# An interleave of two arrays: x in four tiles of 64 KiB rows in one buffer, y in column halves

## The chip, the cores and the metric

The kernel runs on one core of one Trainium2 chip. The metric is the device time of one execution, in microseconds, as the median of several runs. The core has a TensorE, a VectorE (DVE in the profile), a ScalarE (ACT), a GpSimd (POOL) and a SyncE (SP); this kernel computes on VectorE alone, and uses SP and ACT to issue transfers. The transfers run on 16 DMA engines that both issuing queues share. A tile in on-chip memory has 128 partitions; a "row" below is the stretch of one partition that one DMA moves, contiguous in HBM and on the chip.

## The reference

Two float32 arrays of shape 32 x 256 x 1024 are interleaved element by element along the last axis:

```
result = np.zeros((batch, seq, dim * 2), dtype=np.float32)
result[..., 0::2] = x
result[..., 1::2] = y
```

So 33.55 MB of x and 33.55 MB of y are read, and 67.11 MB are written. There is no arithmetic. Since the whole array is interleaved in the same manner, it may be cut anywhere as one flat sequence.

## The kernel before

The flat arrays are cut into n = 8 tiles of 128 partitions with W = 8192 floats each (32 KiB per partition, 4 MiB per tile of x and of y). Row p of tile k is contiguous in HBM, and the rows of a tile lie one behind another. The output of a tile is 64 KiB per partition; it is produced in two halves h of 32 KiB each, so that a store writes 32 KiB of every 64 KiB.

There are two buffers each for x (`xt`), y (`yt`) and output halves (`ot`), every one 32 KiB per partition; all six take 192 KiB of a partition.

Three engines work through lists of their own, which are written out by hand, and meet only in semaphores:

- SP issues all loads (lines 42 to 53), in the order x, y of each tile. From the third tile on, the load of x waits until the third of the four copies of the tile two before is done (L48, semaphore `woven`, which every copy raises by one), and that of y until the fourth is (L52): then the buffer is free. Tile 0's x comes as two halves (L42, L43), whose two DMAs are moved ahead of the barrier that opens the program (lines 103 to 122), so that they run before the other engines are ready.
- VectorE does two copies for each output half, x into the even columns (L67) and y into the odd ones (L70). Before the first of them it waits for the x tile, and for the earlier store from the same output buffer (`osem`); before the second, for the y tile.
- ACT issues a store as soon as both copies of a half are done (L74 and L83). The very first half goes out as two stores, of 8 and 24 KiB per partition (L77, L81), with a semaphore of its own, `qsem`, for the first.

Within a queue the DMAs are served in the order of issue. Loads are on one queue (q1 in the profile), stores on another (q10). Where both have work, each of the 16 engines alternates between them row by row: in the trace a 32 KiB row of a load is followed by a 32 KiB row of a store. A DMA is complete when, on each engine, a small record behind its eight rows has been served; that is what raises the semaphore.

The kernel ends when the last two stores have landed (L87 to L93).

Of the kernel before, what the change touches and what calls it, by code (L numbers as in the profile page):

```python
# [3 lines left out]


def _interleave(nc, x, y, out):
    P = 128
    W = 8192
    H = W // 2  # L10

    total = 1
    for s in x.shape:
        total *= s
    n = total // (P * W)
    assert n * P * W == total

    def rows(ap, names, k):
        flat = ap.rearrange("b s d -> (b s d)")
        return flat[k * names : (k + 1) * names].rearrange("(p w) -> p w", p=P)  # L20

    fp32 = mybir.dt.float32
    xt = [nc.alloc_sbuf_tensor(f"xt{b}", [P, W], fp32).ap() for b in (0, 1)]
    yt = [nc.alloc_sbuf_tensor(f"yt{b}", [P, W], fp32).ap() for b in (0, 1)]
    ot = [nc.alloc_sbuf_tensor(f"ot{b}", [P, W], fp32).ap() for b in (0, 1)]

    xsem = [nc.alloc_semaphore(f"xsem{b}") for b in (0, 1)]
    hsem = nc.alloc_semaphore("hsem")
    qsem = nc.alloc_semaphore("qsem")
    ysem = [nc.alloc_semaphore(f"ysem{b}") for b in (0, 1)]  # L30
    woven = nc.alloc_semaphore("woven")
    osem = [nc.alloc_semaphore(f"osem{b}") for b in (0, 1)]


    cuts = [0, W // 4, W]
    parts = [slice(a, b) for a, b in zip(cuts, cuts[1:])]

    xs = [rows(x, P * W, k) for k in range(n)]
    ys = [rows(y, P * W, k) for k in range(n)]
    os_ = [rows(out, 2 * P * W, k) for k in range(n)]  # L40

    nc.sync.dma_start(out=xt[0][:, :H], in_=xs[0][:, :H]).then_inc(xsem[0], 16)  # L42
    nc.sync.dma_start(out=xt[0][:, H:], in_=xs[0][:, H:]).then_inc(hsem, 16)  # L43

    for k in range(n):
        b = k % 2
        if k >= 2:
            nc.sync.wait_ge(woven, 4 * (k - 2) + 3)  # L48
        if k:
            nc.sync.dma_start(out=xt[b], in_=xs[k]).then_inc(xsem[b], 16)  # L50
        if k >= 2:
            nc.sync.wait_ge(woven, 4 * (k - 2) + 4)  # L52
        nc.sync.dma_start(out=yt[b], in_=ys[k]).then_inc(ysem[b], 16)

    for k in range(n):
        b = k % 2
        for h in (0, 1):
            c = slice(h * H, (h + 1) * H)
            if h == 0:
                nc.vector.wait_ge(xsem[b], 16 * (k // 2 + 1))  # L60
            elif k == 0:
                nc.vector.wait_ge(hsem, 16)
            if k:
                nc.vector.wait_ge(osem[h], 16 * k)
            if (k, h) == (1, 0):
                nc.vector.wait_ge(qsem, 16)
            nc.vector.tensor_copy(out=ot[h][:, 0::2], in_=xt[b][:, c]).then_inc(woven, 1)  # L67
            if h == 0:
                nc.vector.wait_ge(ysem[b], 16 * (k // 2 + 1))
            nc.vector.tensor_copy(out=ot[h][:, 1::2], in_=yt[b][:, c]).then_inc(woven, 1)  # L70

    for k in range(n):
        for h in (0, 1):
            nc.scalar.wait_ge(woven, 4 * k + 2 * h + 2)  # L74
            if (k, h) == (0, 0):
                for c in parts[:-1]:
                    nc.scalar.dma_start(  # L77
                        out=os_[k][:, c], in_=ot[h][:, c]
                    ).then_inc(qsem, 16)
                c = parts[-1]  # L80
                nc.scalar.dma_start(out=os_[k][:, c], in_=ot[h][:, c]).then_inc(osem[h], 16)  # L81
                continue
            nc.scalar.dma_start(  # L83
                out=os_[k][:, h * W : (h + 1) * W], in_=ot[h]
            ).then_inc(osem[h], 16)

    nc.scalar.wait_ge(osem[0], 16 * n)  # L87
    used = sorted(s.num for s in [*xsem, hsem, qsem, *ysem, woven, osem[0]])
    assert used == list(range(used[0], used[-1] + 1)), used
    nc.scalar.sem_clear(range(used[0], used[-1] + 1))  # L90
    nc.sync.nop(nofuse=True).wait_op(osem[1], 16 * n, "sem-ge").then_inc(
        osem[1], -16 * n
    )  # L93


def kernel(tc, x, y, out):
    nc = tc.nc
    tc.close()
    tc.compile()

    _interleave(nc, x, y, out)

    blocks = nc.main_func.blocks
    for engine in (mybir.EngineType.SP, mybir.EngineType.SP):
        opening = blocks[0].instructions
        at, moved = next(
            (b, i)
            for b in blocks[1:]
            for i in b.instructions
            if i.engine == engine and i.opcode == "DMACopy"  # L110
        )
        assert not (moved.sync_info and moved.sync_info.on_wait)
        body = at.instructions
        body.remove(moved)
        gate = next(
            n
            for n, i in enumerate(opening)
            if i.engine == engine and i.opcode == "Drain"
        )
        opening.insert(gate, moved)  # L120
        at.instructions = body
        blocks[0].instructions = opening


# [1 line left out]
_INS = ['x', 'y']  # L126
_OUTS = [((32, 256, 2048), 'float32')]


# [23 lines left out]
```

## Time and profile before

The three runs took 314.12, 314.23 and 314.33 us; the median is 314.23.

| | before |
|---|---|
| median of the runs | 314.23 us |
| the profiled execution's own time | 314.18 us |
| its span (first to last instruction) | 312.9 us |
| VectorE busy | 72.0 us (23%), 32 copies |
| loads (q1): rows and completion records, MB, share of 16 engines | 2448, 67.11, 50.1% |
| stores (q10): the same | 2448, 67.11, 49.7% |
| mean traffic over the span | 429 GB/s |
| VectorE idle before L67, waiting for stores | 206.5 us |
| VectorE idle before L70, waiting for y (once) | 12.3 us |
| first copy starts, first store issued | 7.33 us, 24.24 us |

How to read it: the span is the time from the first to the last instruction that the profiler saw; the execution takes a little longer. "DMA share" is the mean busy share of the 16 DMA engines in a stretch. The chain that ended last is followed backwards from the last instruction, at each step to what released it. Waiting times of an engine are put to what ended them. Idle time of VectorE costs nothing as such; what counts is whether the DMA engines have work. Over a short stretch the GB/s waver by some per cent, since a row is counted where it starts or ends.

### The profile page before, as it was taken

To read this page: it belongs to the slowest core of one execution; us is meant where nothing else is said; L and a number is where in the kernel's file an instruction comes from. 1 tells how busy PE (TensorE), PEld (TensorE's weight loads), DVE (VectorE), ACT (ScalarE), POOL (GpSimd) and SP (SyncE) were. 2 spreads that over 40 slices of the span, in tenths; PEclk is the share of its full clock that TensorE was granted. 3 is DMA by queue.
4 is the path that set the end of the run, shared out by engine and by line. 5 is a ranking of instruction groups with operands and counts; after the bars stand their busy time and mean duration, and the time that the engine had idled before them with its cause. 6 is when DMAs were issued, how large, how long until landed. Compare 5 with 4: busy or idle time off the path is not lost.

```text
span 312.9 us, 114 instructions
## 1 busy us (share of the span) xinstructions
DVE 72.0 (23%) x32; POOL 0.2 (0%) x4
## 2 busy tenths in 40 slices
DVE  0216000501305023050220503205032050415410
POOL 0000000000000000000000000000000000000000
DMA  8999999999999999999999999999999999999998
GB/s 337 467 402 436 436 402 419 452 457 415 427 444 411 461 402 469 402 469 402 469 402 465 406 440 432 423 448 402 469 402 469 402 469 402 469 402 448 423 423 381
DMA packets 4896, 134.22 MB, mean 429 GB/s; under 512 B 544, under 2 KB 544, under 8 KB 544
## 3 DMA queue, kind: packets, MB, share of 16 engines
q1 hardware_dynamic: 2448, 67.11, 50.1%
q10 hardware_dynamic: 2448, 67.11, 49.7%
HBM read 67.11 MB, written 67.11 MB: 429 GB/s over the span
## 4 chain that ended last, share of the span: by engine, by line
DMA 82%; DVE 12%; issue 0%
DMA out_dram<-ot 76%; DMA yt<-in_y_dram 6%; DVE ot L70 6%; DVE ot L67 6%
## 5 line engine op out<-in xcount | busy, mean ns | idle before, releaser
L67 DVE COPY ot<-xt 128x4096 f32<-128x4096 f32 x16 | 36.7, 2295 | 213.8 <-DMA out_dram<-ot 206.5
L70 DVE COPY ot<-yt 128x4096 f32<-128x4096 f32 x16 | 36.6, 2288 | 12.3 <-DMA yt<-in_y_dram 12.3
L137 POOL MEMSET const-bfloat16-1.0<- 128x1 bf16 x1 | 0.1, 103 | 0.0
L137 POOL MEMSET const-uint8-127<- 128x1 uint8 x1 | 0.1, 102 | 0.0
L137 POOL MEMSET const-float32-0.0<- 128x1 f32 x1 | 0.1, 100 | 0.2 <-issue 0.2
L137 POOL MEMSET const-float32-1.0<- 128x1 f32 x1 | 0.1, 99 | 0.0
## 6 DMA issues: line engine op xcount, KB each, us to landing
out_dram<-ot ACTq DMA_DIRECT2D x15, 4096.0 KB, 34.1
yt<-in_y_dram SPq DMA_DIRECT2D x8, 4096.0 KB, 41.5
xt<-in_x_dram SPq DMA_DIRECT2D x7, 4096.0 KB, 24.3
xt<-in_x_dram SPq DMA_DIRECT2D x2, 2048.0 KB, 9.5
out_dram<-ot ACTq DMA_DIRECT2D x1, 3072.0 KB, 32.8
out_dram<-ot ACTq DMA_DIRECT2D x1, 1024.0 KB, 16.3
```

The costliest lines, as they stand in the source:

```text
L67: nc.vector.tensor_copy(out=ot[h][:, 0::2], in_=xt[b][:, c]).then_inc(woven, 1)
L70: nc.vector.tensor_copy(out=ot[h][:, 1::2], in_=yt[b][:, c]).then_inc(woven, 1)
L137: nc = _bacc.Bacc("TRN2", target_bir_lowering=False, num_devices=1)
```

## The change

W becomes 16384, so there are n = 4 tiles of 64 KiB per partition for x and y each. x has one buffer of 64 KiB instead of two of 32, and each tile of x is loaded by one DMA with rows of 64 KiB. A tile of y comes as two column halves of 32 KiB per partition, each into a buffer of its own. The output of a tile is now 128 KiB per partition, and goes out in four quarters of 32 KiB, alternately from two buffers. All buffers together still take 192 KiB of a partition, and every copy still has 128 x 4096 elements.

The order of the loads is new. In the opening, x of tile 0 and the first half of y stand ahead of the opening barrier, in place of two halves of x; y's second half follows behind it. For every later tile SP waits for the fourth of the eight copies of the tile before and loads y's first half, waits for the seventh (the last that reads x) and loads x, waits for the eighth and loads y's second half. The very first store is cut in 8 and 24 KiB as it was. Rows of stores lie 128 KiB apart in HBM instead of 64, and rows of y 64 KiB apart instead of 32.

```diff
-    W = 8192
+    W = 16384
     H = W // 2
+    Q = W // 4
...
-    xt = [nc.alloc_sbuf_tensor(f"xt{b}", [P, W], fp32).ap() for b in (0, 1)]
-    yt = [nc.alloc_sbuf_tensor(f"yt{b}", [P, W], fp32).ap() for b in (0, 1)]
-    ot = [nc.alloc_sbuf_tensor(f"ot{b}", [P, W], fp32).ap() for b in (0, 1)]
+    xt = nc.alloc_sbuf_tensor("xt", [P, W], fp32).ap()
+    yt = [nc.alloc_sbuf_tensor(f"yt{b}", [P, H], fp32).ap() for b in (0, 1)]
+    ot = [nc.alloc_sbuf_tensor(f"ot{b}", [P, H], fp32).ap() for b in (0, 1)]
...
-    nc.sync.dma_start(out=xt[0][:, :H], in_=xs[0][:, :H]).then_inc(xsem[0], 16)
-    nc.sync.dma_start(out=xt[0][:, H:], in_=xs[0][:, H:]).then_inc(hsem, 16)
     for k in range(n):
-        b = k % 2
-        if k >= 2:
-            nc.sync.wait_ge(woven, 4 * (k - 2) + 3)
         if k:
-            nc.sync.dma_start(out=xt[b], in_=xs[k]).then_inc(xsem[b], 16)
-        if k >= 2:
-            nc.sync.wait_ge(woven, 4 * (k - 2) + 4)
-        nc.sync.dma_start(out=yt[b], in_=ys[k]).then_inc(ysem[b], 16)
+            nc.sync.wait_ge(woven, 8 * (k - 1) + 4)
+            nc.sync.dma_start(out=yt[0], in_=ys[k][:, :H]).then_inc(ysem[0], 16)
+            nc.sync.wait_ge(woven, 8 * (k - 1) + 7)
+        nc.sync.dma_start(out=xt, in_=xs[k]).then_inc(xsem, 16)
+        if k:
+            nc.sync.wait_ge(woven, 8 * (k - 1) + 8)
+        else:
+            nc.sync.dma_start(out=yt[0], in_=ys[k][:, :H]).then_inc(ysem[0], 16)
+        nc.sync.dma_start(out=yt[1], in_=ys[k][:, H:]).then_inc(ysem[1], 16)
...
+        for h in range(4):
+            j = 4 * k + h
+            o = ot[j % 2]
             if h == 0:
-                nc.vector.wait_ge(xsem[b], 16 * (k // 2 + 1))
+                nc.vector.wait_ge(xsem, 16 * (k + 1))
+            if j >= 2:
+                nc.vector.wait_ge(osem[j % 2], 16 * (j // 2))
+            if j == 2:
+                nc.vector.wait_ge(qsem, 16)
+            nc.vector.tensor_copy(
+                out=o[:, 0::2], in_=xt[:, h * Q : (h + 1) * Q]
+            ).then_inc(woven, 1)
+            if h % 2 == 0:
+                nc.vector.wait_ge(ysem[h // 2], 16 * (k + 1))
+            c = (h % 2) * Q
+            nc.vector.tensor_copy(
+                out=o[:, 1::2], in_=yt[h // 2][:, c : c + Q]
+            ).then_inc(woven, 1)
...
+    cuts = [0, H // 4, H]
+    for j in range(4 * n):
+        dst = os_[j // 4][:, (j % 4) * H : (j % 4 + 1) * H]
+        nc.scalar.wait_ge(woven, 2 * j + 2)
+        parts = [slice(a, b) for a, b in zip(cuts, cuts[1:])] if j == 0 else [slice(0, H)]
+        for c in parts[:-1]:
+            nc.scalar.dma_start(out=dst[:, c], in_=ot[j % 2][:, c]).then_inc(qsem, 16)
+        c = parts[-1]
+        nc.scalar.dma_start(out=dst[:, c], in_=ot[j % 2][:, c]).then_inc(osem[j % 2], 16)
```

In the prediction, L42, L44 and L47 are lines of the kernel after: the waits of SP ahead of y's first half, of x and of y's second half.

More of the change, by code (lines that the diff above doesn't have):

```diff
@@ L22, in _interleave @@
     fp32 = mybir.dt.float32
-    xt = [nc.alloc_sbuf_tensor(f"xt{b}", [P, W], fp32).ap() for b in (0, 1)]
-    yt = [nc.alloc_sbuf_tensor(f"yt{b}", [P, W], fp32).ap() for b in (0, 1)]
-    ot = [nc.alloc_sbuf_tensor(f"ot{b}", [P, W], fp32).ap() for b in (0, 1)]
-    xsem = [nc.alloc_semaphore(f"xsem{b}") for b in (0, 1)]
-    hsem = nc.alloc_semaphore("hsem")
+    xt = nc.alloc_sbuf_tensor("xt", [P, W], fp32).ap()
+    yt = [nc.alloc_sbuf_tensor(f"yt{b}", [P, H], fp32).ap() for b in (0, 1)]
+    ot = [nc.alloc_sbuf_tensor(f"ot{b}", [P, H], fp32).ap() for b in (0, 1)]
+    xsem = nc.alloc_semaphore("xsem")
     qsem = nc.alloc_semaphore("qsem")
@@ L32, in _interleave @@
     osem = [nc.alloc_semaphore(f"osem{b}") for b in (0, 1)]
-    cuts = [0, W // 4, W]
-    parts = [slice(a, b) for a, b in zip(cuts, cuts[1:])]
     xs = [rows(x, P * W, k) for k in range(n)]
@@ L55, in _interleave @@
+            nc.sync.dma_start(out=yt[0], in_=ys[k][:, :H]).then_inc(ysem[0], 16)
[6 more added lines that the diff above has]
+        nc.sync.dma_start(out=yt[1], in_=ys[k][:, H:]).then_inc(ysem[1], 16)
     for k in range(n):
-        b = k % 2
-        for h in (0, 1):
-            c = slice(h * H, (h + 1) * H)
+        for h in range(4):
+            j = 4 * k + h
+            o = ot[j % 2]
@@ L59, in _interleave @@
             if h == 0:
-                nc.vector.wait_ge(xsem[b], 16 * (k // 2 + 1))
[L61 to L65, printed above, removed]
-                nc.vector.wait_ge(qsem, 16)
[L67 to L85, printed above, removed]
@@ L87, in _interleave @@
-    nc.scalar.wait_ge(osem[0], 16 * n)
-    used = sorted(s.num for s in [*xsem, hsem, qsem, *ysem, woven, osem[0]])
+                nc.vector.wait_ge(xsem, 16 * (k + 1))
+            if j >= 2:
+                nc.vector.wait_ge(osem[j % 2], 16 * (j // 2))
+            if j == 2:
+                nc.vector.wait_ge(qsem, 16)
+            nc.vector.tensor_copy(
[3 more added lines that the diff above has]
+                nc.vector.wait_ge(ysem[h // 2], 16 * (k + 1))
@@ L89, in _interleave @@
+    nc.scalar.wait_ge(osem[0], 32 * n)
+    used = sorted(s.num for s in [xsem, qsem, *ysem, woven, osem[0]])
     assert used == list(range(used[0], used[-1] + 1)), used
     nc.scalar.sem_clear(range(used[0], used[-1] + 1))
-    nc.sync.nop(nofuse=True).wait_op(osem[1], 16 * n, "sem-ge").then_inc(
-        osem[1], -16 * n
+    nc.sync.nop(nofuse=True).wait_op(osem[1], 32 * n, "sem-ge").then_inc(
+        osem[1], -32 * n
     )
```

## The prediction

> **What bounds the kernel now.** I read the page's utilisation rows first, then its chain, then the chain in order of time, then a table of busy time by stretch, and last the order of instructions at the end. From the page, DMA busy tenths and traffic:
>
> ```profile
> DMA  8999999999999999999999999999999999999998
> HBM read 67.11 MB, written 67.11 MB: 429 GB/s over the span
> ```
>
> From the first slice to the last the 16 DMA engines are busy. The page's chain that ended last agrees:
>
> ```profile
> DMA 82%; DVE 12%; issue 0%
> DMA out_dram<-ot 76%; DMA yt<-in_y_dram 6%; DVE ot L70 6%; DVE ot L67 6%
> ```
>
> VectorE's 12% in that chain is no time to be won: the DMA row does not dip while it weaves. A piece of the chain in order of time (start, length, what):
>
> ```profile
> 81.36 34.17 DMA out_dram<-ot
> 115.53 0.02 issue
> 115.55 2.29 DVE ot L67
> 117.85 2.21 DVE ot L70
> 120.06 0.02 issue
> 120.08 34.17 DMA out_dram<-ot
> ```
>
> The step repeats every 38.72 us (81.36 to 120.08), in which 16.78 MB move: two loads and two stores of 4 MiB. So one 4 MiB transfer costs the engines 38.72 / 4 = 9.68 us; I call this one unit. Busy time by stretch (bounds and length, VectorE, POOL, clock, DMA share, GB/s):
>
> ```profile
> 26.00:32.00 6.00, 2.61 (x2) 0.00 (x0) 1.00 0.99 395
> 32.00:42.00 10.00, 0.00 (x0) 0.00 (x0) 1.00 1.01 432
> 115.55:154.28 38.73, 9.00 (x5) 0.00 (x0) 1.00 1.00 433
> ```
>
> The steady rate is 433 GB/s; only where the first store joins the loads (26 to 32) is it lower: 6 x (433 - 395) / 433 = 0.5 us lost, once. At the end, in order of time, stores run alone:
>
> ```profile
> 283.90 2.30 DVE L67 COPY ot<-xt 128x4096 f32<-128x4096 f32 x1 [8.95 <-DMA out_dram<-ot]
> 286.11 2.29 DVE L70 COPY ot<-yt 128x4096 f32<-128x4096 f32 x1
> 293.53 2.29 DVE L67 COPY ot<-xt 128x4096 f32<-128x4096 f32 x1 [5.14 <-DMA out_dram<-ot]
> ```
>
> Two stores land 9.63 us apart: stores alone run at the mixed rate, and so do loads alone (the first y tile's 4 MiB took 9.68 us by the trace's records of single rows). So it does not matter which queue has work, only that one has. The span can be summed: 32 units x 9.68 = 309.8; 1.0 before the first row moves; 0.9 of slow first rows; 0.6 lost as stores join (those 0.5, and 0.1 near 41 us); 0.1 for the shorter rows of the first load and store; 0.1 for engines that end at different times; 0.35 from the last row to its semaphore. Together 312.85, against 312.9. The profiled execution took 314.18, 1.3 more than its span, and stands 0.05 under the median of 314.23.
>
> **The change part by part.** *Work.* The bytes and the 32 VectorE copies (2.29 us each) are the same, so the 32 units stay. Stores keep their 17 DMAs; loads go from 17 to 12. In the records a 32 KiB row takes 1213 ns, a 16 KiB row 611, an 8 KiB row 309: joining two rows saves 2 x 611 - 1213 = 9 ns (4 ns by the spacing of whole transfers). Each engine moves 72 rows of x before and 32 after: 40 joins, 0.16 to 0.36 us; five completion records of 9 ns fewer, 0.05. Saved: 0.2 to 0.4, I take 0.25. For a 64 KiB row there is no record; below, it could be cut back into 32 KiB rows (then only the 8 joins in the first tile and the records stay, 0.1), and nothing in the straight line from 8 to 32 KiB says that 64 leaves it.
>
> *Start.* Two loads (8 MiB x, 4 MiB y) instead of two of 2 MiB now stand ahead of the opening barrier; the third, y's second half, follows at about 1.9, where L53 issues now. Loads alone run from 1.0. x lands at about 1.9 + 2 units + 0.3 = 21.7, y0's half at 31.4, and the first store is issued at 33.7 instead of 24.24. That costs nothing while loads cover it: four units of loads last until 1.9 + 38.7 = 40.6, and 24.24 to its first row at 28.64 shows 4.4 us of delay for the store, so rows at 38.1. Cover left: 2.5 us. If it were gone, each us of lateness would cost one.
>
> *Where the single x buffer empties the load queue.* SP's order is now y first half (after the tile's second weave), x (after the seventh copy), y second half (after the eighth). SP waits for VectorE at L42, L44 and L47; behind each wait only later loads are queued, and it is VectorE that needs those. In tile 0, y's next first half is issued at 38.2, starts at about 42 and shares with stores 1:1 until 55.7. Then no load exists until the x buffer is free. The stores go on alone: the rest of store 0 to 60.2, store 1 to 69.9; store 2 is issued one landing and one weave after 60.2 (0.3 + 4.5, as 283.90 to 288.4), at 65.0, and 1.0 later can move (0.00 to 0.99, the first load). Needed at 69.9, there at 66.0: 3.9 us of cover, as in the tail above. Were it gone, the engines would idle for the excess, up to three times.
>
> *x returns.* Store 1 lands at 70.2, the seventh copy ends at 72.5, x is issued. Now the load's rows of 64 KiB alternate with the store's of 32. In the steady part rows alternate singly (a store takes 19.36 us there, two units), so x gets two thirds: 2 units / (2/3) = 3 units = 29 us, from about 76 to 105. Stores get one unit in that time, and have stores 2 and 3, nearly 1.5 units, left: they run until 112. Store 4 needs x (105.2) and a weave (109.8), and is there 1.4 us before store 3 ends; besides, y's second half (issued at 74.7, queued behind x) keeps loads going until 124. Two covers, so nothing is lost. If the row is cut in two, x gets half, lands at about 109, the stores run out at 104, and y's second half alone bridges until store 4 comes at 114.5: still no gap. The following tiles repeat with eight units, 77.4 us.
>
> *End.* x's last load lands near 260, y's half near 279; stores 13, 14 and 15 run alone at 9.68 against a weave of 4.5, as they do now. Nothing.
>
> *Price that the trace does not show: a queue that has run dry and starts again.* In before, each queue starts once and never runs dry. The stores' one start cost 0.5 us. In after the load queue restarts three times (x of tiles 1, 2, 3). Bounds: zero (the start of a new DMA in a queue that has work, as at 77 or 116, shows nothing) and 3 x 0.5 = 1.5. A restart could also gain nothing below zero, since the engines are full. I take zero: the 0.5 spreads over rows from 26 to 32 us and later joins of a new transfer have none, which looks like a first use rather than a fee per start; but this is the weakest step.
>
> *Spacing in HBM.* Output rows of 32 KiB now lie 128 KiB apart instead of 64, y's 64 instead of 32. From x and y (32) to out (64) today's rate does not change, 9.68 in both, so I take zero. The Trainium skill, "DMA: Bandwidth & Descriptors", section "Latency and other measured facts", speaks against this: row pitches at large powers of two slow HBM copies, 207 GB/s at a pitch of 512 KiB where a padded layout had 214. This trace shows no such loss, at a pitch of at most 64 KiB; by that 3.3% on the 24 units of y and out my estimate would be 7.7 us more.
>
> Sum: 312.9 - 0.25 = 312.6 of span, + 1.3 = 313.95. I forecast **314.0 us**, 0.1% under before. A measurement of this kernel can tell about 0.2% (0.6 us) from no change.
>
> **The rivals.** *1. Restarts cost (slower).* Place: just after 72, 150 and 227 us, where x's load joins running stores. Price 0.5 each, 314.0 + 1.5 = 315.5. It decides from (0.6 + 0.2) / 3, about 0.3 each. For it: the only two starts in the trace, the first load's and the first store's, both lost time. Against it: the first start has nothing before it, and the second may be first use.
>
> *2. The wider pitch slows stores and y's loads (slower).* Each per cent on 24 units is 24 x 9.68 x 1% = 2.3 us, 316.3. For it no row of this case; against it that doubling from 32 to 64 KiB costs nothing today.
>
> *3. Both queues run dry at 66 to 70 us (slower).* If a store needed its 4.4 us from issue to first row even with no load in the way, store 2 would be there at 69.4, still before 69.9; another us of delay, three times, gives 316.
>
> *4. Rows are not joined.* x of 64 KiB moves as two rows: x lands 36 us after its issue instead of 33, time 314.1, no change.
>
> *5. Faster.* If 64 KiB rows save their full 0.4 and the first store's join loses nothing: 314.2 - 0.4 - 0.5 = 313.3.
>
> **How the numbers follow.** Forecast with joined rows 0.45 and rival 4, same time, 0.14: 0.59 within 0.2%. Rival 1 at 0.3 us or more each 0.26, rival 2 0.05, rival 3 0.03: slower 0.34. Rival 5: faster 0.07. The range goes from 313.5 (rival 5 in part) to 315.6 (rival 1 in full), which leaves out rivals 2 and 3 and the far part of 5, some 0.13. The likeliest case alone would span 313.7 to 314.4.
>
> **What the profile after would show.** DMA in nines throughout; 433 GB/s from 115 to 250; VectorE's first-copy waits moved partly to x's landing, four times; x landing 33 us after issue (36 if cut in two); some 4,180 DMA packets (4,690 if cut). Right or wrong on restarts: the rate from 72 to 80, 150 to 158 and 227 to 235 is 433 or visibly below. Weaves at the start of a tile 77.4 us apart; a longer step beside full DMA tenths is rival 2, beside a dip is 3. The forecast is wrong if any stretch of the engines idles, or if a unit no longer costs 9.68.

## The result, and the profile after

The changed kernel took 314.56 us (median of 22 runs, 314.25 to 315.58) against 314.26 for the kernel before (22 runs, 314.12 to 314.42): a ratio of 1.0017, with a 95% interval of 1.0010 to 1.0024. It is 0.3 us slower where 0.3 faster was forecast. What stands out is the scatter: before, 22 runs lie within 0.3 us; after, 12 lie between 314.25 and 314.57 and ten between 314.89 and 315.58. The execution that was profiled is one of the upper ten: 315.29 us, with a span of 314.0.

The page of the kernel after, DMA busy tenths, packets and traffic:

```profile
DMA  9999999999999899999999989999999999999997
DMA packets 4176, 134.22 MB, mean 428 GB/s; under 512 B 464, under 2 KB 464, under 8 KB 464
HBM read 67.11 MB, written 67.11 MB: 427 GB/s over the span
```

The DMA row is nearly as full as before, and 4176 packets are the number forecast for rows of 64 KiB that move as one. The chain that ended last is nearly that of before:

```profile
DMA 83%; DVE 12%; issue 0%; SPq 0%
DMA out_dram<-ot 73%; DMA yt<-in_y_dram 10%; DVE ot L68 6%; DVE ot L62 6%; SPq L45 0%
```

VectorE's waits, and the x transfers of the page's list of DMA issues (count, microseconds from issue to landing):

```profile
DVE ot L62 <- DMA xt<-in_x_dram: 114.7, 4, 31.1
DVE ot L62 <- DMA out_dram<-ot: 105.0, 11, 23.2
```
```profile
xt<-in_x_dram SPq DMA_DIRECT2D x4, 33.0
```

Waiting moved from stores to x, four times, and x lands 33 us after its issue, both as forecast. The steady rate is the same. Stretches of the kernel after (bounds and length, VectorE, POOL, clock, DMA share, GB/s):

```profile
115.00:250.00 135.00, 30.37 (x14) 0.00 (x0) 1.00 1.01 434
311.50:312.00 0.50, 0.00 (x0) 0.00 (x0) 1.00 0.30 131
312.00:312.50 0.50, 0.00 (x0) 0.00 (x0) 1.00 0.32 131
```

and the same stretches of the kernel before:

```profile
115.00:250.00 135.00, 31.48 (x14) 0.00 (x0) 1.00 1.01 434
311.50:312.00 0.50, 0.00 (x0) 0.00 (x0) 1.00 0.00 0
312.00:312.50 0.50, 0.00 (x0) 0.00 (x0) 1.00 0.02 0
```

434 GB/s from 115 to 250 us in both. The difference is in the last two lines. A row is counted where it starts; 131 GB/s over 0.5 us are 65 KB, two rows of 32 KiB. So in after four rows start after 311.5 us, on single engines, while the others have nothing left. In before no row starts so late. So the lost time of this run lies not in the steady rate but in how far apart the engines end.

The trace's records of single rows say how far. The last store's completion records come on the 16 engines from 312.24 to 312.48 us in before, and from 312.16 to 313.58 in after. The first engine is 0.08 us earlier; the last is 1.10 later, and the span grew by 1.1. From the first loads to 308 us the engines of after hardly idle (0.02 us, summed over all 16). What sets them apart is single rows that take longer than the usual time for their size (1213 ns for 32 KiB, 2418 for 64); I call them late rows. In before there is none between 43 and 300 us. In after nearly all of them are loads, on a few engines at a time. The larger ones are 0.3 and 0.4 us late at 78, 0.4 at 134, 0.3 at 233, 0.3 at 263 and 0.3 at 270 us; smaller ones stand near these, and at 50 us.

The time between the first and the last of the 16 engines to finish a store is called the spread below. In before it is 0.24 us from 57 us to the end. In after it is 0.53 us at 70 us, when the stores run alone for the first time, 1.35 at 148 and at 225 us, and 1.42 at the end. So in this run most of the extra spread arises after the opening, at the first restart of x (78 us) and in the transfers that follow it.

The prediction had named the rate at the three restarts as a test. From 72 to 80, 150 to 158 and 227 to 235 us after shows 410, 455 and 455 GB/s, and before 426, 459 and 451, where it has no restart: stretches this short waver by more than what is looked for.

The end of after, in order of time, answers to the tail of before; the stores run alone at 9.67 us each, only later:

```profile
284.93 2.29 DVE L62 COPY ot<-xt 128x4096 f32<-128x4096 f32 x1 [11.39 <-DMA out_dram<-ot]
294.60 2.29 DVE L62 COPY ot<-xt 128x4096 f32<-128x4096 f32 x1 [5.17 <-DMA out_dram<-ot]
```

### The profile page after: what moved, and what is told of

The parts are those of the page before. It is cut to its first block, busy times and chain, and to the rows that moved or that the text cites. A ratio compares the mean times of both kernels' runs of the same rounds, so it can differ in the third digit from the quotient of the medians.

```text
span 314.0 us, 106 instructions
## 1 busy us (share of the span) xinstructions
DVE 72.0 (23%) x32; POOL 0.2 (0%) x4
## 2 busy tenths in 40 slices
DMA packets 4176, 134.22 MB, mean 428 GB/s; under 512 B 464, under 2 KB 464, under 8 KB 464
## 4 chain that ended last, share of the span: by engine, by line
DMA 83%; DVE 12%; issue 0%; SPq 0%
DMA out_dram<-ot 73%; DMA yt<-in_y_dram 10%; DVE ot L68 6%; DVE ot L62 6%; SPq L45 0%
## 5 line engine op out<-in xcount | busy, mean ns | idle before, releaser
L62 DVE COPY ot<-xt 128x4096 f32<-128x4096 f32 x16 | 36.7, 2295 | 219.7 <-DMA xt<-in_x_dram 114.7
```

Source lines behind the costliest of these rows:

```text
L62: nc.vector.tensor_copy(out=o[:, 0::2], in_=xt[:, h * Q : (h + 1) * Q]).then_inc(woven, 1)
```

## The experiments

"Dry" below means that a queue holds nothing on an engine until a later transfer starts it again; "the opening" is the time up to the first stores; "the join" is the stretch in which the first store's rows come in beside running loads. Each result is a median with its lowest and highest run, and then the ratio to the kernel before on the same chip, with its 95% interval. Where no number of runs is given there were 11 or 12. In the code, "..." stands for lines left out; semaphores and waits that only follow from an edit are left out too. Each kernel has a short name (a1, b1 and so on).

**First round: which part of the change.** a1, the changed kernel with the 64 KiB rows undone:

```diff
-        nc.sync.dma_start(out=xt, in_=xs[k]).then_inc(xsem, 16)
+        for c in (slice(0, H), slice(H, W)):
+            nc.sync.dma_start(out=xt[:, c], in_=xs[k][:, c]).then_inc(xsem, 16)
...
-                nc.vector.wait_ge(xsem, 16 * (k + 1))
+                nc.vector.wait_ge(xsem, 32 * (k + 1))
```

> The changed kernel with each x tile loaded as two transfers of 32 KiB rows, issued back to back into the same single buffer; nothing else differs. Theory R (the restart of a dry load queue costs single rows, whatever their length): as the changed kernel, 314.5 with runs scattered up to 315.5, and slow load rows again just after the restarts. Theory L (64 KiB rows cause it, by alternating with 32 KiB rows of stores): 314.2 with a scatter of 0.3 as before, and the engines end within 0.25 us of each other instead of 1.4.

314.70 us (314.39 to 316.69), 1.0026 [1.0013, 1.0040]. Rows of 64 KiB are not needed for the loss or the scatter. More changed than the rows, though: two halves of x now stand ahead of the opening barrier, x lands later (109.8 instead of 106.6 us), and the store queue is dry for about 15 us three times, where it is for 2 to 4.6 us in the changed kernel. The profiled run (314.59, one of the shorter) has its late rows at 50, at 134 to 137 and at 214 to 217 us, not right behind the restarts of x (77, 155 and 232), so theory R as worded isn't borne out either.

b1, the spacing in HBM alone, on the kernel before:

```diff
         flat = ap.rearrange("b s d -> (b s d)")
-        return flat[k * names : (k + 1) * names].rearrange("(p w) -> p w", p=P)
+        pair = flat[k // 2 * 2 * names : (k // 2 + 1) * 2 * names]
+        w = names // P
+        return pair.rearrange("(p w) -> p w", p=P)[:, k % 2 * w : (k % 2 + 1) * w]
```

> The kernel before, with its 32 KiB rows taken at the wide spacing of the changed kernel: loads 64 KiB apart, stores 128 KiB apart; buffers, order and queues as before. Theory P (the spacing costs, above all where the first store joins the loads): the loss at the join grows from 0.5 to 0.8 us per engine, time 314.5 or more. Theories R and L: 314.2 as before, join 0.5.

314.32 us (314.20 to 314.45), 1.0002 [0.9993, 1.0011]. Stores 128 KiB apart cost nothing that can be measured. The late rows at the join came to 0.76 us per engine against 0.55 in before, without a longer time.

b2, three dry load queues, on the kernel before:

```diff
-            nc.sync.wait_ge(woven, 4 * (k - 2) + 3)
+            nc.sync.wait_ge(woven, 4 * (k - 1) + 2 if k in (2, 4, 6) else 4 * (k - 2) + 3)
...
-        if k >= 2:
+        if k >= 2 and k not in (2, 4, 6):
```

> The kernel before, with the loads of tiles 2, 4 and 6 held back until the first half of the tile before them is woven, so that the load queue runs dry three times while stores go on; rows and spacing as before. Theory R: slow load rows after each restart, engines that end up to 1 us apart, 314.5 to 315.5. Theories L and P: 314.2, no slow rows after 42 us.

318.81 us (318.44 to 319.78, 4 runs), 1.0150 [1.0137, 1.0163]: more than asked for. At 138 and 217 us the store queue ran out at about the same moment, and nearly all 16 engines lost up to 1.5 us on one row each; the spread at the end is 2.0. That is no clean test of a covered restart. It was repeated with one tile (e1, below).

a2, the first store whole, on the changed kernel (`cuts = [0, H]`, and without the wait on `qsem`):

> The changed kernel with its first store in one piece of 32 KiB rows instead of 8 and 24. If the join's loss (0.8 us per engine, of which part stays with single engines) comes from the short first rows: 314.2 or a little under, engines within 0.6 us at the first stores. If it comes from the start of the store queue as such: 314.5 and scattered as the changed kernel, join 0.8.

315.32 us (315.24 to 315.41, 5 runs), 1.0034 [1.0022, 1.0046]. The short first rows are not to blame. In its trace the first rows of the first store start on the 16 engines from 38.83 to 41.20 us.

**Second round: the late first store, or the turns later on.** c1, the late start alone, on the kernel before:

```diff
-        nc.sync.dma_start(out=yt[b], in_=ys[k]).then_inc(ysem[b], 16)
+        for m in {0: [], 1: [0, 1]}.get(k, [k]):
+            nc.sync.dma_start(out=yt[m % 2], in_=ys[m]).then_inc(ysem[m % 2], 16)
```

> The kernel before with one change: the first y tile is loaded behind the second x tile, so that the first store is issued at about 34 us, as in the changed kernel, instead of 24; buffers, rows and the steady order are those of before. Theory J (the later start of the stores sets the excess and the scatter): loss at the join 0.8 us per engine, engines up to 0.5 us or more apart from there on, 314.5 to 315.5. Theory T (the turns later on, where one queue starts again or the row sizes that alternate change, set it): 314.3, engines 0.25 to 0.35 apart to the end.

314.20 us (314.12 to 315.10), 1.0009 [1.0000, 1.0018]; six runs at 314.12 to 314.20, five at 314.75 to 315.10, neither theory's picture. The join lost no more than before (0.5 us), so lateness as such is not it. The load queue had, without my seeing it beforehand, run dry once, from 73.7 to 87.0 us; in the profiled run (314.98) the first late rows after the join stand right there, at 87 to 95.

d1, an early start on the changed kernel, x of tile 0 in two column halves with y's first half between:

```diff
-        nc.sync.dma_start(out=xt, in_=xs[k]).then_inc(xsem, 16)
+        c = slice(0, H if k == 0 else W)
+        nc.sync.dma_start(out=xt[:, c], in_=xs[k][:, c]).then_inc(xsem, 16)
...
             nc.sync.dma_start(out=yt[0], in_=ys[k][:, :H]).then_inc(ysem[0], 16)
+            nc.sync.dma_start(out=xt[:, H:], in_=xs[k][:, H:]).then_inc(hsem, 16)
```

> The changed kernel with x of tile 0 in two column halves and y's first half loaded between them, so that the first store is issued at 24 us as in before; everything from tile 1 on is as changed. Theory J: loss at the join 0.5, 314.0 to 314.2, scatter 0.3. Theory T: join 0.5, but slow single load rows after the restarts of x remain, engines over 0.6 us apart at the end in most runs, 314.4 to 315.

315.50 us (315.13 to 315.71, 5 runs), 1.0042 [1.0030, 1.0054]. Theory J falls: the first store is as early as in before, and the time is longer. The late rows stand at 78, 115, 156, 212, 234, 247 and 271 us.

e1, one dry moment on the kernel before (the edit of b2 for k = 4 only):

> The kernel before with the loads of tile 4 alone held back until the first half of tile 3 is woven, so that the load queue runs dry once, between about 122 and 138 us, with stores queued. Theory T: slow load rows on single engines within some 10 us of the restart or at the next turns, engines 0.5 to 1.5 us apart afterwards, 314.4 to 315.5. Theory J: no slow rows after 42 us, 314.25.

315.98 us (314.68 to 316.59, 6 runs), 1.0052 [1.0038, 1.0067]. Until 155 us its trace is as quiet as before's, with a spread of 0.38; after the restart at 138 and that of the stores at 184 us it is 0.8 to 1.2, and 2.6 at the last store but two. There a new loss comes in: since the next weave waits for the slowest engine, the store queue runs out on the others (0.9 us of idle engines near 293 us). Part of this price is thus a second effect. Still, with the opening of before, holding back one tile's loads cost some 1.7 us in the median.

after_again, the changed kernel once more, for a second trace:

> The changed kernel once more, for a second trace. If the end is set by the slowest engine, the span exceeds 312.7 by about as much as the engines' spread at the last store exceeds 0.24 us, and the first engine to end is at 312.1 to 312.4 again, whatever the run's time.

316.30 us, span 315.0 (one run, longer than any of the 22 above). Only the spread came as expected, 1.69 at the last store: the first engine ended at 312.91, not at 312.1 to 312.4, and the span exceeds 312.7 by 2.3, more than the spread explains. Here x's restart in the last tile cost nearly every engine, 0.7 us on average, near 237 to 242 us. It is the price that rival 1 gave to every restart, in one of the six that two traces of this kernel show.

**Third round: what a dry queue does, apart from rows.** f1, the load queue kept filled, on the changed kernel: x in halves, the first reloaded early:

```diff
+            nc.sync.wait_ge(woven, 8 * (k - 1) + 3)
+            nc.sync.dma_start(out=xt[:, :H], in_=xs[k][:, :H]).then_inc(xsem[0], 16)
             nc.sync.wait_ge(woven, 8 * (k - 1) + 4)
...
-        nc.sync.dma_start(out=xt, in_=xs[k]).then_inc(xsem, 16)
+        else:
+            nc.sync.dma_start(out=xt[:, :H], in_=xs[k][:, :H]).then_inc(xsem[0], 16)
+        nc.sync.dma_start(out=xt[:, H:], in_=xs[k][:, H:]).then_inc(xsem[1], 16)
```

> The changed kernel with x loaded in column halves of 32 KiB rows, the first half again as soon as its two copies are done (after the third of the eight copies), so that the load queue always holds a transfer; the opening stays late and the spacing wide as in the changed kernel. Against a1_rows32 only the moment of one load per tile differs. Theory T (losses come at the restarts and turns that the single buffer brings): no slow rows after the opening, engines no further apart at the end than at 60 us, 314.2 to 314.4, at worst the scatter of c1_latejoin. If the late opening or the spacing carries the rest after all: 314.6 and scattered to 315.5 as a1_rows32.

314.43 us (314.17 to 315.78), 1.0009 [1.0000, 1.0019]. In the median better than a1, which has the same opening and more dry stretches, though the two intervals overlap; still scattered; and the load queue did run dry once, from 73.3 to 87.2, because of the late opening. In its profiled run (315.78) the late rows stand at 87 to 95 again; from 112 to 267 us the spread stays at 2.55, and it is 1.84 once the loads are over.

h1, rows of 16 KiB in one load of the kernel before, without a dry queue (tile 4's x as two column halves):

> The kernel before with tile 4's x loaded in two halves of 16 KiB rows; by the walk of the two queues neither runs dry, but for some 15 us rows of 16 and 32 KiB alternate instead of 32 and 32, once in the middle of the run. If any change in what alternates costs rows on single engines: slow load rows near 120 to 160 us, engines 0.4 to 1.2 us apart after it, 314.4 to 315. If only a queue that runs dry does: as before, 314.25, no slow rows after 42 us.

314.30 us (314.14 to 314.50), 1.0001 [0.9992, 1.0010], no late rows after the join, spread 0.44 from 57 us to the end. This change of row sizes alone costs nothing that can be measured.

f2, to have no dry queue at all: f1 with d1's early opening:

> d1_earlyjoin with x in column halves of 32 KiB rows, the first half loaded again after the third of the eight copies of a tile: the opening of d1, the spacing, the y halves and the output quarters of the changed kernel, and no queue that runs dry before the end of the loads. In f1_neverdry and in c1_latejoin the load queue had, against what I expected, run dry once, from 73.3 to 87.2 and from 73.7 to 87.0 us, and slow rows stood right behind it. If a queue that runs dry and starts again is what costs: no slow rows after 45 us, engines under 0.6 us apart from 60 us to the end, 314.2 to 314.4 and no run above 314.6. If some other property of the changed kernel costs: as d1_earlyjoin, 315.1 to 315.7.

314.74 us (314.39 to 317.27), 1.0022 [1.0006, 1.0038]. Not as expected: no queue runs dry, and the runs scatter more than ever. The profiled run (314.42) is a quiet one. The dry queue was not the whole story. But b1, which is quiet, has the same spacing, row sizes and order from the first store on; only the opening differs.

**Fourth round: the opening.** o1, the kernel before with its first load in one piece. With that, two transfers of 4 MiB stand ahead of the barrier, as two large ones do in the changed kernel:

```diff
-    nc.sync.dma_start(out=xt[0][:, :H], in_=xs[0][:, :H]).then_inc(xsem[0], 16)
-    nc.sync.dma_start(out=xt[0][:, H:], in_=xs[0][:, H:]).then_inc(hsem, 16)
+    nc.sync.dma_start(out=xt[0], in_=xs[0]).then_inc(xsem[0], 16)
...
-            elif k == 0:
-                nc.vector.wait_ge(hsem, 16)
```

> The kernel before with tile 0's x in one transfer of 32 KiB rows instead of two of 16 KiB, so that the loads ahead of the barrier are x and y of tile 0; nothing else. Theory O (the rows of the opening decide how the engines come out of the first store's join): join and start lose 1.4 to 1.5 us per engine instead of 1.15, time 314.4 to 314.8, with single runs above 315. If only a queue that runs dry later costs: 314.25, highest 314.5.

314.96 us (314.48 to 316.34), 1.0025 [1.0016, 1.0034]. This edit alone makes the kernel before as slow and as scattered as the changed kernel, or more. Start and join together lost 1.4 us per engine, as expected.

o2, the opening of before put back on the changed kernel (d1, with the first half of x in two transfers of 16 KiB rows):

```diff
-        c = slice(0, H if k == 0 else W)
+        c = slice(0, Q if k == 0 else W)
         nc.sync.dma_start(out=xt[:, c], in_=xs[k][:, c]).then_inc(xsem, 16)
+        if k == 0:
+            nc.sync.dma_start(out=xt[:, Q:H], in_=xs[k][:, Q:H]).then_inc(zsem, 16)
```

> The changed kernel with the opening of before: the first half of tile 0's x in two transfers of 16 KiB rows, then y's first half, x's second half, y's second half; from tile 1 on as changed, with the single buffer and 64 KiB rows. Theory O alone: 314.25, highest 314.6. If the queues that run dry cost by themselves: slow rows behind the restarts at about 78, 155 and 233 us, 314.4 to 315.6.

314.36 us (314.24 to 315.40), 1.0008 [0.9999, 1.0016]; ten of eleven runs at or under 314.60. Its trace has the single buffer, the 64 KiB rows and the restarts at 77, 155 and 232 us, with one late row behind them (0.4 us, at 156) and a spread of 0.42 at the end. Against d1, from which it differs only in the first load and so in what stands ahead of the barrier, 1.1 us are gone and the intervals are far apart; against the changed kernel itself (1.0010 to 1.0024) they just overlap.

b1 and f2 once more, side by side:

> The kernel before at the wide spacing once more, on the same chip as the other three. Both theories: 314.3, highest 314.5, as on the first chip. If it scatters here up to 315, it is the chip that scatters, and the comparison of f2 with b1 says nothing on the opening.

314.32 us (314.14 to 314.44), 1.0004 [0.9995, 1.0012]: quiet again.

> f2_early_neverdry once more, beside b1_again: the two differ in the opening alone (first load in one transfer of 32 KiB rows against two of 16, and y's first half ahead of the barrier). Theory O: 314.5 to 314.8 with runs above 315 again. If the first result was the chip's: as b1_again.

314.88 us (314.27 to 317.23), 1.0023 [1.0009, 1.0037], beside b1_again on one chip. So the scatter belongs to the kernel and not to the chip, and since the two differ in the opening alone, to its opening.

What the opening does can be seen in the list of the DMA queues over a short stretch, 28.3 to 29.8 us, in which the first store's first 8 KiB row follows a load's row. The kernel before:

```profile
q1 hardware_dynamic: 16, 0.52, 87.7%
q10 hardware_dynamic: 16, 0.13, 20.6%
```

and o1:

```profile
q1 hardware_dynamic: 16, 0.52, 92.4%
q10 hardware_dynamic: 15, 0.12, 19.3%
```

In before all 16 engines (16 packets on q10) take the first store row between the same two load rows. In o1 one engine does not. Its row comes one load row later, at 30.22 us. I call this a split. From the records of all traces (first store: start of its first row, earliest and latest engine; last store: completion on the first engine, plus the spread):

```
kernel        profiled run  first store      last store      a queue dry before the loads end
before        314.18        28.64 to 28.93   312.24 + 0.24   no
b1_pitch      314.25        28.55 to 28.99   312.20 + 0.34   no
b1_again      314.28        28.49 to 28.96   312.24 + 0.36   no
h1_rowmix     314.21        28.49 to 28.96   312.09 + 0.44   no
f2            314.42        28.54 to 29.08   312.35 + 0.38   no
f2_again      314.39        28.52 to 29.05   312.29 + 0.39   no
o2            314.27        28.70 to 29.23   312.16 + 0.42   yes
c1            314.98        38.15 to 38.56   312.11 + 1.18   once
o1            314.96        28.54 to 30.22   312.24 + 1.03   no
after         315.29        38.24 to 40.00   312.16 + 1.42   yes
after_again   316.30        38.28 to 40.02   312.91 + 1.69   yes
a1            314.59        38.25 to 38.73   312.30 + 0.57   yes
a2            315.32        38.83 to 41.20   312.22 + 1.41   yes
d1            315.71        28.54 to 30.25   312.26 + 1.76   yes
f1            315.78        38.11 to 39.60   312.25 + 1.84   once
e1            316.59        28.47 to 28.85   313.73 + 1.16   once, the stores too
b2            318.44        28.50 to 28.88   314.70 + 2.03   three times, the stores too
```

Where the engines take the first store within 0.6 us and no queue runs dry, they end within 0.45 us and the run is under 314.5. Where some take it a row later, they end 1.0 to 1.8 apart. But c1, e1 and b2 have no split, and end 1.2 to 2.0 apart after a dry stretch.

The split is also not the whole of those 1.0 to 1.8 us. In o1 the spread is 0.6 after the join (a load at 46 us), and late rows at 96 and 116 us bring it to 1.03. Six kernels with x's restarts have stores that run alone at about 70, 148 and 225 us, so that their spread can be compared in time:

```
kernel        split   at 70   at 148   at 225   at the last store
o2            no      0.43    0.43     0.42     0.42
a1            no      0.54    0.57     0.57     0.57
after         yes     0.53    1.35     1.35     1.42
after_again   yes     0.83    1.04     1.99     1.69
a2            yes     1.14    1.30     1.30     1.41
d1            yes     0.75    1.26     1.35     1.76
```

In these traces the restarts add to the spread where a split came first, and hardly where none did. At the end, o1 has one engine left over:

```profile
311.50:312.00 0.50, 0.00 (x0) 0.00 (x0) 1.00 0.00 0
312.00:312.50 0.50, 0.00 (x0) 0.00 (x0) 1.00 0.17 66
```

while o2, the changed kernel with the old opening, ends as before does:

```profile
311.50:312.00 0.50, 0.00 (x0) 0.00 (x0) 1.00 0.00 0
312.00:312.50 0.50, 0.00 (x0) 0.00 (x0) 1.00 0.02 0
```

The engines come out of the opening loads 0.39 to 0.52 us apart in the eight traces that start with rows of 16 KiB, and 0.33 to 0.71 apart in the nine that start with 32 or 64 KiB; a split at the first store's first row occurred in none of the former and in six of the latter. That the opening changes the time is shown (o1 beside before, f2 beside b1, o2 beside d1). That it does so through this split is read from the traces and not shown: nothing was run that moves the split alone, the long runs of f2 were not traced, and its two traced runs are quiet and have no split. Nor was anything run that tells the row size of the first load from what stands ahead of the barrier.

## Why the prediction was wrong

The range (313.5 to 315.6) holds the result and the change is within the 0.2% that was called no change, but the sign is wrong. Point by point:

*Work.* Right in kind. A 64 KiB row is one packet of 2418 ns, 8 less than two of 1213. Whether the 0.25 us taken for it was gained the runs do not show: the first engine to end is at 312.16 instead of 312.24, but in h1, which has no 64 KiB row, it is at 312.09.

*Start.* **This is the step that failed.** "That costs nothing while loads cover it" looked only at whether the engines have work, and they had: the first store row came at 38.2 (forecast 38.1) beside running loads. What the step did not ask is whether 16 engines still do the same thing at the same time. With the new opening they often do not (a split in after, after_again and d1, none in o2). With the opening of before in its place (o2) the ratio is 1.0008 instead of 1.0017; a large first load alone, on the kernel before (o1), costs 1.0025 [1.0016, 1.0034].

*The sum's "0.1 for engines that end at different times".* I carried it over from before as a constant. It is the term of the sum that was mis-sized: in the profiled run the spread went from 0.24 to 1.42 us, which is all of that run's loss. Averages over 16 engines hid it: 434 GB/s stands in both.

*x returns.* x's landing (33 us from its issue) was right, and so was the result that no engine idles. The cover of store 4 was mis-sized: I gave a store 1.0 us from issue to first row, from the idle first load. Beside loads it took 3.6 to 4.2 (issued at 111.2, 189.2 and 266.9, first rows at 114.7, 193.4 and 270.6), and x landed 1.4 later than forecast. So the store queue, too, ran dry three times, for 2 to 4.6 us, with y's second half as the only cover. The tiles' first weaves came 78.0 and 77.7 us apart instead of 77.4, the sign that the prediction gave to rival 2; b1 speaks against that rival, and a weave waits for the last of 16 engines, so I put it down to the spread, which is not shown.

*The restart, taken as zero.* Too low as well, and by how much stays open. For a small part: with the opening of before and all restarts (o2) the ratio is 1.0008 with an interval that just takes in 1. For a larger one: e1 (1.0052 from one dry stretch, the opening as in before), c1's five long runs of eleven, d1 against f2 (1.0042 against 1.0022, though f2 also undoes the 64 KiB rows), and the profiled run of after itself, where the spread was 0.53 us before the first restart and 1.35 at 148 us. Rival 1 had the place right but charged all engines at each restart; that occurred at one of the six that were traced. How much of the median's 0.3 us is restarts and how much opening cannot be divided with these runs; the table of spreads suggests that the two act together.

*Spacing in HBM.* Taken as zero, and right: 1.0002 and 1.0004 for b1. The loss that the Trainium skill, "DMA: Bandwidth & Descriptors", section "Latency and other measured facts", gives for row pitches at large powers of two, from 512 KiB up, does not show here at 128 KiB.

*Rival 3* (the queues dry at 66 to 70 us) did not occur: store 2, issued at 66.0, had its first row at 70.3, just as store 1's first engine ended. That was closer than forecast (3.9 us of cover), and since the step rested on the 1.0 us that was too short, it was partly luck that it held.

## What to carry to other kernels

In this kernel, whose DMA engines are full from end to end, the time is that of the slowest of the 16 (in after 313.58 us for the last store's last record, in a span of 314.0), and what one engine lost the others did not make up. Before calling an edit of the opening or of a refill free because "the engines have work", compare how far apart the engines finish a transfer, in several runs: the mean rate did not show it here (434 GB/s in both), the scatter between runs did. The kernel before, in which neither queue runs dry and all engines take up the second queue at the same row, was not beaten by any run with longer rows.

## What the runs showed of the hardware that was not expected

- By estimate, from 32 transfers of 4 MiB at the measured 9.68 us, the moving itself takes 309.8 us, and before stands 3.1 us above that. Row times repeat to a nanosecond for most rows (1213 for 32 KiB; 2418 for 420 of the 512 rows of 64 KiB in after).
- Late rows are nearly always loads, beside stores, mostly 0.1 to 0.5 us each, on a few engines. In o1 they stop at 116 us, and the offsets between engines then stay: a spread of 1.03 from 134 us to the end.
- A store that finds its queue empty while loads run has its first row 3.3 to 4.8 us after its issue, over all traces; the very first load, with nothing else running, 1.0.
- Rows of 64 KiB beside rows of 32 KiB alternate by rows, not by bytes: x took 33 us from issue to landing, 29 of them from its first row (77.5 us) on, which is 3 units of 9.68.
